# Gates of an expert layer: which one-hot operand is moved, and which stands still

## The chip, the cores and the metric

The program runs on one core of a Trainium2 chip. The metric is the device time in microseconds; lower is better. Each kernel is run several times and the median is taken. One more execution is recorded by the hardware profiler, and all views below are of that one.

The engines are named as in the profile: PE is TensorE (matmuls), PEld its loads of the stationary operand, DVE is VectorE, ACT is ScalarE, POOL is GpSimd, SP is SyncE, which here issues DMA transfers.

## The reference, cut to what matters

Two transformer-like blocks on 256 tokens of width 1024. The last layer is a product-key expert layer: each token chooses 16 of 16,384 experts for each of 8 heads, so 128 experts with a weight each. An expert has a number `first * 128 + second`.

```python
def one(xb):                                   # xb: tokens x 1024
    q = (xb @ wq).reshape(C, PEER_HEADS, 2, PEER_DK_HALF)
    s = jnp.einsum('chpd,hpnd->chpn', q, keys)
    sv, si = lax.top_k(s, K)
    ...
    top_s, sel = lax.top_k(cand.reshape(C, PEER_HEADS, K * K), K)
    eidx = jnp.take_along_axis(cidx.reshape(C, PEER_HEADS, K * K), sel, axis=-1)
    g = jax.nn.softmax(top_s, axis=-1)
    u = u_tab[eidx]
    act = jax.nn.gelu(jnp.einsum('chkd,cd->chk', u, xb), approximate=False)
    w = (g * act).astype(xb.dtype)
    return jnp.einsum('chk,chkd->cd', w, v_tab[eidx])
```

## The kernel before

The kernel does not gather experts. In `peer` it multiplies all 16,384 rows of `u` with all tokens (128 pieces of 128 experts, `u_items`), multiplies each activation by a gate that is zero for experts not chosen, and multiplies the result with all rows of `v` (`v_chunk`). The gates are a tile `G[second number, first number, token]` in float32, and the change is in how it is filled.

**Routing** (`route`) finds for each token its 128 chosen experts and leaves them in `slot[chosen, 5, token]`, in bfloat16: row 0 the first number, row 1 the second, rows 2 to 4 the weight in three parts that add up to it exactly.

**Filling the gates** goes in groups of NB = 4 tokens, 64 groups. `build(t0)` makes one tile `oo[chosen, 5, 128, 4]` on DVE with two instructions. Line 1203 compares the numbers 0 to 127 with the first and the second number of each chosen expert: two sets of one-hot rows, 1024 elements a partition. Line 1204 multiplies the first number's one-hots by the three parts of the weight: 1536 elements. `place(t0)` then does for each of the four tokens three matmuls on PE (line 1212), one for each part of the weight, which add up in PSUM: out[second, first] = sum over the chosen experts of onehot(second) x onehot(first) x weight. The stationary operand is `oo[:, 1, :, j]`, the moving one `oo[:, x, :, j]`, 128 x 128 each. The tokens are the last dimension of `oo`, so that neighbouring columns of an operand are 4 elements, 8 bytes, apart. ACT copies the result of a group into `G` (line 1214). `oo` has two buffers and the PSUM pool `ps_t` three.

**What runs beside it.** `weave(U[NRT:NU], gates(), True)` spreads the 64 builds and 64 places over 53 pieces of `u` (numbers 72 to 124). One piece is: a transfer of 512 KB into `raw` (four buffers, line 127, issued by SP), ACT's copy to a rounded `hi` (line 128, three buffers), DVE's rest `lo` (line 129, two buffers), and 24 matmuls of 256 columns on PE (`mm_a`, lines 139 to 141: `hi` twice, `lo` once). Every second piece ACT applies Gelu (line 1076). The list of gates begins with `build(0)`, and then goes `build(t0 + 4)`, `place(t0)`, so that a build is one place ahead of its own place. By the counts 53 pieces and 64 places, one or two places stand behind a piece. The last argument of `weave` asks that DVE takes up a build only behind the split (line 129) of the same piece. Ahead of this stretch the routing of the first 72 pieces keeps DVE busy; behind it three more pieces follow and then the 128 pieces of `v` (line 1254).

Of the kernel before, what the change touches and what calls it, by code (L numbers as in the profile page):

```python
# [16 lines left out]
OP = mybir.AluOpType  # L17
# [49 lines left out]
def tile_body(ctx, tc, A, out):  # L67
# [12 lines left out]

    # ---- constants
    scratch = tc.tile_pool(name="scratch", bufs=1)
# [33 lines left out]

    # ---- weights: load a piece, split it exactly in two parts of 12 significant bits
    last, crit = [None, None], [None, None]
# [68 lines left out]
    def sum_sq(t, c, o, src, eps):  # L187
        # mean of squares of a row, in two halves
        s = stat[:, t, o:o + 3]
        crit[1] = nc.scalar.activation(sqs, src, AF.Square, accum_out=s[:, c:c + 1])  # L190
        if c == 0:
            nc.vector.tensor_scalar(s[:, 2:3], s[:, 0:1], 1.0 / D, eps, op0=OP.mult, op1=OP.add)
        else:
            nc.vector.tensor_scalar(s[:, 2:3], s[:, 1:2], 1.0 / D, s[:, 2:3], op0=OP.mult, op1=OP.add)
# [24 lines left out]
    def both_norms(t, c, acc):  # L219
        # the residual times the first block's last gain, the means of squares of both, and from these  # L220
        # 1 / rms of the first norm and the product of that with 1 / rms of the norm that follows it
        if c == 0:
            gains["sum", t] = npool.tile([P, D], F32, name="hn")
        a, b, st = gains["sum", t][:, cut(c)], h[t][:, cut(c)], stat[:, t]
        crit[0] = nc.vector.tensor_tensor(a, acc, b, op=OP.add)
        nc.vector.tensor_tensor(b, a, gains["final_g"][:, cut(c)], op=OP.mult)
        sum_sq(t, c, 0, a, EPS)
        sum_sq(t, c, 3, b, 0.0)
        if c:
            nc.vector.scalar_tensor_tensor(st[:, 6:7], st[:, 2:3], EPS, st[:, 5:6], op0=OP.mult, op1=OP.add)  # L230
            nc.vector.tensor_copy(st[:, 7:8], st[:, 2:3])
            nc.gpsimd.tensor_tensor(st[:, 6:8], st[:, 6:8], nhalf[:, :2], op=OP.pow)

    def keep_tiles(pool, n, *names):
        # made when first written; names: slots of tiles that are not read any more by then
        return [lambda name=name: pool.tile([P, 2, PIECE], F32R, name=name, bufs=1)
                for name in [*names, *(f"keep{j}" for j in range(n - len(names)))]]

    def out_proj(src, nk, yT, keep, fin=residual):
        """The last pieces are kept, so that the first tokens are done before the others."""  # L240
        acc = [ps_mm.tile([P, 512], F32, name="mm") for _ in range(4)]
# [31 lines left out]
    def defer(f, n=1):  # L273
        """Emit a step after the n-th of the items that follow."""
        late.append([n, f])
# [17 lines left out]
    def weave(items, side, behind=False):  # L293
        """Emit a list of steps with a list of smaller ones spread between them, by their costs.

        behind: VectorE takes up the smaller ones only behind the split of the step's weights.
        """
        side = [f if isinstance(f, tuple) else (1.0, f) for f in side]
# [16 lines left out]
    def causal(ps, acc, taps, cw, cb):  # L315
        # causal convolution along the tokens; the last tap has no shift
        nc.scalar.activation(acc, ps, AF.Identity, scale=cw[:, taps - 1:taps], bias=cb)  # L317
# [24 lines left out]
    def b_first(src, xT, pool, evac):  # L342
        """A block that begins on the first tokens while the others are still on their way."""
        W = [weight(src[q], 2, keep=pool.tile([P, 2, PIECE], F32R, name=f"keep{q - 2}", bufs=1) if q > 1 else None)
# [9 lines left out]
        def turn(f):  # L354
            # two of its four blocks of columns, columns on partitions
            pt = ps_t.tile([P, 2, T], F32, name="pst")
# [7 lines left out]
    def row_parts(pool, rows, name):  # L364
        # a table that is there twice, at partitions 0 and 32: its first part at 0, its second at 32
        n = rows.shape[0]
# [5 lines left out]
    def rowbc(ps, rows, r, more=None):  # L372
        # one row of a table in two parts, on all partitions; more: a tile to add
        n = rows.shape[0]
# [17 lines left out]

    # ---- layer 0: state space mixer
    def ssd():
        with ExitStack() as es:
# [46 lines left out]
            nc.vector.tensor_scalar(nacs, tk[:, 1], -1.0, None, op0=OP.mult)  # L442
            # large and negative where the position read comes after the position written
            jm = sb.tile([P, P], F32, name="jm")
# [31 lines left out]
            def xs_items(g):  # L476
                # inputs of the recurrence, tokens on partitions
                hs = slice(8 * g, 8 * g + 8)
# [22 lines left out]
            def chain(g):  # L501
                hs = slice(8 * g, 8 * g + 8)
                # decay between every two positions of a chunk, transposed, times the masked products of B and C
                M = {}
# [20 lines left out]
                def state():  # L525
                    # state after the first chunk, read by the second
                    xds = sb.tile([P, 512], F32, name="xds", bufs=2)
# [96 lines left out]
    def fox():  # L624
        with ExitStack() as es:
# [45 lines left out]
            nc.vector.tensor_tensor_scan(cum, one, lf, 0.0, op0=OP.mult, op1=OP.add)  # L671
            # cum is minus the reference's sum
            cumr = row_parts(sb, cum, "cumr")
# [41 lines left out]
            def attend(hg):  # L715
# [3 lines left out]
                def scores(i, pr):  # L719
# [7 lines left out]
                    mx = sb.tile([P, 2], F32, name="mx", bufs=3)  # L727
                    # minus the scores, and minus their maximum
                    for j, hh in enumerate(pr):
# [52 lines left out]
    def mix2():  # L782
        with ExitStack() as es:
# [13 lines left out]

            # convolution branch: some of the taps on the tensor engine, as diagonal matrices
            cT = sb.tile([P, 4, T], F32, name="cT")
# [36 lines left out]

            # low-rank query and key-value parts, tokens on partitions
            cqT = sb.tile([P, 2, 2, T], F32R, name="cqT")
# [12 lines left out]
            def norm_later(src, dst, g, n, then, half=False):  # L851
                # half: the source is twice the row that is meant
                w = src.shape[-1]
# [107 lines left out]
            def scores(i, hh):  # L961
# [4 lines left out]
                mx = sb.tile([P, 1], F32, name="mx", bufs=3)  # L966
                # minus the scores, and minus their maximum
                nc.vector.tensor_tensor_reduce(z[:, :n], sp[:, :n], amask[:, TM - n:], scale=-scale, scalar=-NEG,
# [45 lines left out]
            def conv_done(t):  # L1014
# [12 lines left out]
                def rest():  # L1027
                    nc.vector.scalar_tensor_tensor(ln, ln, r, lb, op0=OP.mult, op1=OP.add)
                    # x (1 + tanh(x / 2)) is twice silu(x)
                    th = sb.tile([P, 512], F32, name="on", bufs=2)  # L1030
# [23 lines left out]
    def peer():  # L1054
        with ExitStack() as es:
# [26 lines left out]
            with ExitStack() as e1:  # L1082
# [8 lines left out]
                def route(t):  # L1091
# [59 lines left out]
                    def finish():  # L1151
# [8 lines left out]
                        for j in range(3):  # L1160
                            nc.tensor.transpose(pt[:, j, :], sl[:, j, :], ident)
                        # a bfloat16 holds a row's number; a weight takes three, which hold it exactly
                        cur = slot[:, :, t * P:(t + 1) * P]
# [33 lines left out]
            iob = const.tile([P, P, NB], BF16, name="metaT")  # L1197
            nc.vector.tensor_copy(iob, iota[:, :, None].to_broadcast([P, P, NB]))

            def build(t0):  # L1200
                oo = wk.tile([P, 5, P, NB], BF16, name="oo", bufs=2)
                cur = slot[:, :, None, t0:t0 + NB].to_broadcast([P, 5, P, NB])
                nc.vector.tensor_tensor(oo[:, :2], iob[:, None].to_broadcast([P, 2, P, NB]), cur[:, :2], op=OP.is_equal)
                nc.vector.tensor_tensor(oo[:, 2:], oo[:, :1].to_broadcast([P, 3, P, NB]), cur[:, 2:], op=OP.mult)  # L1204
                O[t0] = oo

            def place(t0):
                pg = ps_t.tile([P, NB, P], F32, name="pst")
                oo = O.pop(t0)
                for j in range(NB):  # L1210
                    for x in range(2, 5):
                        nc.tensor.matmul(pg[:, j, :], lhsT=oo[:, 1, :, j], rhs=oo[:, x, :, j], start=(x == 2),  # L1212
                                         stop=(x == 4))
                nc.scalar.activation(G[:, :, t0:t0 + NB].rearrange("p i t -> p t i"), pg, AF.Copy)  # L1214
# [8 lines left out]

            # the last groups of four rows of experts come first: they are still on chip
            rows = [4 * n + j for n in (30, 31, *range(30)) for j in range(4)]

            def prepare(k, hi, lo):
                # four rows of experts: activation times gate, in two parts
                i = rows[k]
# [83 lines left out]
def _twice(w):  # L1313
    # columns 0.. and, once more, 32..
    o = np.zeros((w.shape[0], P), w.dtype)
# [80 lines left out]
```

## Time and profile before

| | |
|---|---|
| runs | 1769.67, 1768.04, 1768.36 us; median 1768.36 |
| profiled execution, span | 1767.2 us |
| PE busy | 1728.7 us (98%) |
| PE loads busy | 1536.4 us (87%) |
| DVE busy | 1244.6 us (70%) |
| ACT busy | 973.6 us (55%) |
| line 1212, PE | 768 matmuls, 1160.2 to 1395.9 us |
| granted clock of TensorE, mean | 0.997 |

The span is the time from the first to the last instruction of the profiled execution. Busy time of PE is the union of the matmuls' spans, which overlap one another: a matmul's reported duration is longer than the distance from its start to the next one's. For what a matmul costs in a row of many, the distance is read (the time of a group divided by its count), not the duration. Lines are those of the kernel before; a row shows the line, the engine, the operation, the tiles written and read, the count and the times.

### The profile page before, as it was taken

To read this page: it belongs to the slowest core of one execution; us is meant where nothing else is said; L and a number is where in the kernel's file an instruction comes from. 1 tells how busy PE (TensorE), PEld (TensorE's weight loads), DVE (VectorE), ACT (ScalarE), POOL (GpSimd) and SP (SyncE) were. 2 spreads that over 40 slices of the span, in tenths; PEclk is the share of its full clock that TensorE was granted. 3 is DMA by queue.
4 is the path that set the end of the run, shared out by engine and by line. 5 is a ranking of instruction groups with operands and counts; after the bars stand their busy time and mean duration, and the time that the engine had idled before them with its cause. 6 is when DMAs were issued, how large, how long until landed. Compare 5 with 4: busy or idle time off the path is not lost.

```text
span 1767.2 us, 28831 instructions
## 1 busy us (share of the span) xinstructions
PE 1728.7 (98%) x11035; PEld 1536.4 (87%) x11035; DVE 1244.6 (70%) x2516; ACT 973.6 (55%) x1425; POOL 35.2 (2%) x45
## 2 busy tenths in 40 slices
PE   7999999999999999999999999999999999999998
PEld 6978779987777899878979999999999988888886
DVE  5777667765755677667877999977667666666665
ACT  5778546544465565457854544555555544444443
POOL 0000000000110000000000000000000000000000
PEclk9999999999999999999999999999999999999999
DMA  5534346665454465654245676754454577777774
GB/s 192 175 104 144 119 144 181 189 200 181 131 167 132 125 186 183 204 185 141 80 166 172 214 225 224 224 179 140 142 156 134 167 252 237 237 237 238 238 237 156
DMA packets 87578, 315.29 MB, mean 178 GB/s; under 512 B 9984, under 2 KB 10368, under 8 KB 87312
## 3 DMA queue, kind: packets, MB, share of 16 engines
q1 hardware_dynamic: 80352, 290.36, 52.8%
q10 hardware_dynamic: 7088, 23.09, 3.5%
q8 instruction: 86, 1.41, 0.3%
q14 instruction: 52, 0.43, 0.1%
HBM read 295.59 MB, written 17.83 MB: 177 GB/s over the span
## 4 chain that ended last, share of the span: by engine, by line
PE 91%; DVE 4%; ACT 1%; issue 1%; DMA 1%; POOL 1%; SPq 0%; DVEq 0%; POOLq 0%; ACTq 0%
PE mm L1254 20%; PE mm L139 13%; PE mm L141 13%; PE mm L140 13%; PE mm L146 7%; PE mm L145 7%; PE mm L147 7%; PE pst L1212 5%; DVE lo L129 1%; PE pst L171 1%; PE pst L546 1%; PE pst L724 1%; PE pst L375 1%; PE pst L377 1%; PE po L749 1%
## 5 line engine op out<-in xcount | busy, mean ns | idle before, releaser
L129 DVE TENSOR_TENSOR lo<-raw,hi 128x1024 fp32r<-128x1024 f32 (+1 forms) x492 | 599.9, 1220 | 341.7 <-PE mm L141 112.9
L128 ACT ACTIVATE hi<-raw 128x1024 fp32r<-128x1024 f32 (+1 forms) x492 | 519.3, 1057 | 526.0 <-PE mm L140 242.1
L139 PE MATMUL mm<-xT,hi 128*128 128x256 f32 (+1 forms) x1968 | 562.6, 286 | 1.2 <-DVE cacc L320 1.2
L141 PE MATMUL mm<-xT,lo 128*128 128x256 f32 (+1 forms) x1968 | 557.1, 283 | 1.5 <-DVE lo L129 1.5
L140 PE MATMUL mm<-xT,hi 128*128 128x256 f32 (+1 forms) x1968 | 552.0, 281 | 0.0
L139 PEld LDWEIGHTS mm<-xT,hi 128*128 128x128 f32 x1968 | 373.0, 190 | 5.0 <-issue 2.3
L141 PEld LDWEIGHTS mm<-xT,lo 128*128 128x128 f32 x1968 | 370.7, 188 | 2.6 <-DVE lo L129 2.2
L140 PEld LDWEIGHTS mm<-xT,hi 128*128 128x128 f32 x1968 | 371.8, 189 | 0.5
L1254 PE MATMUL mm<-hi,xT 128*128 128x512 f32 x992 | 270.0, 393 | 0.0
L1254 PEld LDWEIGHTS mm<-hi,xT 128*128 128x128 f32 x992 | 186.3, 188 | 42.6
L1254 PE MATMUL mm<-lo,xT 128*128 128x512 f32 x496 | 154.8, 393 | 0.0
L1254 PEld LDWEIGHTS mm<-lo,xT 128*128 128x128 f32 x496 | 93.1, 188 | 21.7 <-DVE lo L129 0.3
L145 PE MATMUL mm<-hi,xT 128*128 128x512 f32 (+1 forms) x240 | 96.3, 408 | 3.9 <-ACT xT L133 3.8
L1212 PE MATMUL pst<-oo 128*128 128x128 bf16 x768 | 99.4, 297 | 0.0
L147 PE MATMUL mm<-hi,xT 128*128 128x512 f32 (+1 forms) x240 | 95.0, 397 | 2.1 <-DVE xT L134 2.1
L146 PE MATMUL mm<-lo,xT 128*128 128x512 f32 (+1 forms) x240 | 96.1, 400 | 0.7 <-DVE lo L129 0.6
L1212 PEld LDWEIGHTS <-oo 128*128 128x128 bf16 x768 | 83.3, 118 | 3.4
L1214 ACT ACTIVATE G<-pst 128x512 f32<-128x512 f32 x64 | 71.1, 1111 | 16.4 <-PE pst L1212 16.4
L320 DVE SCALAR_TENSOR_TENSOR cacc<-mm,pcol,cacc 128x255 f32<-128x255 f32 (+1 forms) x144 | 68.4, 480 | 13.6 <-ACT cacc L317 11.2
L1204 DVE TENSOR_TENSOR oo<-oo,slot 128x1536 bf16<-128x1536 bf16 x64 | 60.2, 956 | 1.4
L145 PEld LDWEIGHTS mm<-hi,xT 128*128 128x128 f32 x240 | 45.5, 191 | 14.3 <-ACT xT L133 5.4
L147 PEld LDWEIGHTS mm<-hi,xT 128*128 128x128 f32 x240 | 45.5, 190 | 12.3 <-DVE xT L134 4.1
(404 smaller groups left out, 2095.7 us busy)
## 6 DMA issues: line engine op xcount, KB each, us to landing
raw<-in_u SPq DMA_DIRECT2D x128, 512.0 KB, 3.7
raw<-in_v SPq DMA_DIRECT2D x128, 512.0 KB, 4.2
raw<-in_w_up SPq DMA_DIRECT2D x88, 512.0 KB, 3.6
raw<-in_w_dn SPq DMA_DIRECT2D x44, 512.0 KB, 4.2
raw<-in_w_fox SPq DMA_DIRECT2D x32, 512.0 KB, 4.2
spill<-h ACTq DMA_DIRECT2D x30, 512.0 KB, 5.4
h<-spill SPq DMA_DIRECT2D x30, 512.0 KB, 4.7
raw<-in_w_xbc SPq DMA_DIRECT2D x24, 512.0 KB, 3.9
```

Source lines behind the costliest of these rows:

```text
L128: last[1] = nc.scalar.activation(hi[:, :width], raw[:, :width], AF.Copy)
L129: last[0] = nc.vector.tensor_tensor(lo[:, :width], raw[:, :width], hi[:, :width].bitcast(F32), op=OP.subtract)
L139: nc.tensor.matmul(ps, lhsT=hi[:, k, :], rhs=xT[:, k, 0, :], start=(k == 0), stop=False)
L140: nc.tensor.matmul(ps, lhsT=hi[:, k, :], rhs=xT[:, k, 1, :], start=False, stop=False)
L141: nc.tensor.matmul(ps, lhsT=lo[:, k, :], rhs=xT[:, k, 0, :], start=False, stop=(k == nk - 1))
L145: nc.tensor.matmul(ps, lhsT=xT[:, k, 0, c0:c1], rhs=whi, start=first, stop=False)
L146: nc.tensor.matmul(ps, lhsT=xT[:, k, 0, c0:c1], rhs=wlo, start=False, stop=False)
L147: nc.tensor.matmul(ps, lhsT=xT[:, k, 1, c0:c1], rhs=whi, start=False, stop=last)
L320: nc.vector.scalar_tensor_tensor(acc[:, d:], ps[:, :T - d], cw[:, j:j + 1], acc[:, d:], op0=OP.mult, op1=OP.add)
L1212: nc.tensor.matmul(pg[:, j, :], lhsT=oo[:, 1, :, j], rhs=oo[:, x, :, j], start=(x == 2), stop=(x == 4))
L1214: nc.scalar.activation(G[:, :, t0:t0 + NB].rearrange("p i t -> p t i"), pg, AF.Copy)
L1254: nc.tensor.matmul(acc[2 * t + c], lhsT=w[x][:, t * P:(t + 1) * P], rhs=y[:, c, :], start=(i == 0 and x == 0 and y is b[0]), stop=(i == P ...
```

## The change

The roles of the two one-hots are exchanged, and one of them gets another layout. The first number's one-hots are made for the four tokens one after the other, 128 neighbouring elements each, in a view `om` of the first fifth of the tile `oo`; for that the numbers 0 to 127 are also kept once in bfloat16 (`ioc`). The second number's one-hots stay in the old layout, and it is these that are multiplied by the three parts of the weight. In `place` the products are the stationary operand and `om[:, j]` is the moving one. The comparison of 1024 elements becomes two of 512. What is summed for each element of `G` is the same.

```diff
+            ioc = pb.tile([P, P], BF16, name="ioc")
+            nc.vector.tensor_copy(ioc, iota)
...
             def build(t0):
                 oo = wk.tile([P, 5, P, NB], BF16, name="oo", bufs=2)
-                cur = slot[:, :, None, t0:t0 + NB].to_broadcast([P, 5, P, NB])
-                nc.vector.tensor_tensor(oo[:, :2], iob[:, None].to_broadcast([P, 2, P, NB]), cur[:, :2], op=OP.is_equal)
-                nc.vector.tensor_tensor(oo[:, 2:], oo[:, :1].to_broadcast([P, 3, P, NB]), cur[:, 2:], op=OP.mult)
-                O[t0] = oo
+                om = oo[:, 0].rearrange("p a b -> p (a b)").rearrange("p (b a) -> p b a", a=P)
+                cur = slot[:, :, t0:t0 + NB]
+                nc.vector.tensor_tensor(om, ioc[:, None].to_broadcast([P, NB, P]),
+                                        cur[:, 0, :, None].to_broadcast([P, NB, P]), op=OP.is_equal)
+                nc.vector.tensor_tensor(oo[:, 1], iob, cur[:, 1, None].to_broadcast([P, P, NB]), op=OP.is_equal)
+                nc.vector.tensor_tensor(oo[:, 2:], oo[:, 1:2].to_broadcast([P, 3, P, NB]),
+                                        cur[:, 2:, None].to_broadcast([P, 3, P, NB]), op=OP.mult)
+                O[t0] = om, oo

             def place(t0):
                 pg = ps_t.tile([P, NB, P], F32, name="pst")
-                oo = O.pop(t0)
+                om, oo = O.pop(t0)
                 for j in range(NB):
                     for x in range(2, 5):
-                        nc.tensor.matmul(pg[:, j, :], lhsT=oo[:, 1, :, j], rhs=oo[:, x, :, j], start=(x == 2),
-                                         stop=(x == 4))
+                        nc.tensor.matmul(pg[:, j, :], lhsT=oo[:, x, :, j], rhs=om[:, j], start=(x == 2), stop=(x == 4))
```

In the changed kernel the three instructions of a build are lines 1208 (first number), 1210 (second number) and 1211 (products), the matmuls are line 1220, and ACT's copy is line 1221. The rows of PE, ACT, SP and POOL stand in the same order as before. On DVE, a piece with one build and one with two, in the middle of the stretch, stood in this order before (`lo<-raw,hi` is the split of a piece of `u`, `metaT` the slot in which the numbers 0 to 127 lie, each four times):

```order
L129 TENSOR_TENSOR lo<-raw,hi 128x1024
L1203 TENSOR_TENSOR oo<-metaT,slot 128x1024
L1204 TENSOR_TENSOR oo<-oo,slot 128x1536
L129 TENSOR_TENSOR lo<-raw,hi 128x1024
L1203 TENSOR_TENSOR oo<-metaT,slot 128x1024 x2
L1204 TENSOR_TENSOR oo<-oo,slot 128x1536 x2
```

A build is two instructions there, and where two builds stand together both comparisons come ahead of both products. The same two pieces in the changed kernel:

```order
L129 TENSOR_TENSOR lo<-raw,hi 128x1024
L1208 TENSOR_TENSOR oo<-ioc,slot 128x512
L1210 TENSOR_TENSOR oo<-metaT,slot 128x512
L1211 TENSOR_TENSOR oo<-oo,slot 128x1536
L129 TENSOR_TENSOR lo<-raw,hi 128x1024
L1208 TENSOR_TENSOR oo<-ioc,slot 128x512
L1210 TENSOR_TENSOR oo<-metaT,slot 128x512
L1208 TENSOR_TENSOR oo<-ioc,slot 128x512
L1211 TENSOR_TENSOR oo<-oo,slot 128x1536
L1210 TENSOR_TENSOR oo<-metaT,slot 128x512
L1211 TENSOR_TENSOR oo<-oo,slot 128x1536
```

A build is three instructions now; the split stands where it stood, and of two builds the second one's line 1208 comes ahead of the first one's products.

## Rows read from the trace of the kernel before

**Rows 1.** The page: busy time and share; the chain that ended last
```profile
PE 1728.7 (98%) x11035; PEld 1536.4 (87%) x11035; DVE 1244.6 (70%) x2516; ACT 973.6 (55%) x1425; POOL 35.2 (2%) x45
...
PE 91%; DVE 4%; ACT 1%; issue 1%; DMA 1%; POOL 1%; SPq 0%; DVEq 0%; POOLq 0%; ACTq 0%
PE mm L1254 20%; PE mm L139 13%; PE mm L141 13%; PE mm L140 13%; PE mm L146 7%; PE mm L145 7%; PE mm L147 7%; PE pst L1212 5%; DVE lo L129 1%; PE pst L171 1%; PE pst L546 1%; PE pst L724 1%; PE pst L375 1%; PE pst L377 1%; PE po L749 1%
```

**Rows 2.** Tile oo: count, ns min/median/max, first and last start in us, form
```profile
L1212 PEld LDWEIGHTS <-oo x768: 112/117/144, 1160.2 to 1395.9; 128*128 128x128 bf16 x192
L1212 PE MATMUL pst<-oo x768: 284/297/302, 1160.2 to 1396.0; 128*128 128x128 bf16 x192
L1203 DVE TENSOR_TENSOR oo<-metaT,slot x64: 689/693/695, 1153.0 to 1390.6; 128x1024 bf16<-128x1024 bf16 x64
L1204 DVE TENSOR_TENSOR oo<-oo,slot x64: 950/957/959, 1154.2 to 1391.4; 128x1536 bf16<-128x1536 bf16 x64
```

**Rows 3.** Windows: busy us (count) of each engine, PEclk, DMA share, GB/s
```profile
1080.00:1153.00 73.00, 73.00 (x619) 73.00 (x619) 69.83 (x396) 36.70 (x42) 0.00 (x0) 1.00 0.73 228
...
1157.00:1398.00 241.00, 241.00 (x2037) 237.57 (x2037) 166.38 (x181) 140.25 (x144) 0.00 (x0) 1.00 0.48 147
```

**Rows 4.** Waits: who for whom, us in total, times, longest; ACT from 1160, DVE from 1080
```profile
ACT hi L128 <- PE mm L140: 83.4, 52, 1.7
...
DVE lo L129 <- PE mm L141: 48.6, 41, 1.2
...
DVE lo L129 <- issue: 8.2, 15, 1.5
```

**Rows 5.** Chain of waits in order of time, line 1212: start, us, what
```profile
1160.40 1.43 PE pst L1212 x12
1164.66 2.84 PE pst L1212 x24
...
1383.50 2.84 PE pst L1212 x24
...
1393.45 2.86 PE pst L1212 x24
```

**Rows 6.** Line 1254: its part of the chain behind the stretch; one matmul's ns
```profile
1405.11 20.02 PE mm L1254 x86
...
L1254 PE MATMUL mm<-hi,xT x992: 388/392/404, 1416.1 to 1759.5; 128*128 128x512 f32 x199
```

**Rows 7.** Timeline around one group: start us, us, engine, line (loads, matmuls, DVE)
```profile
1201.20 0.19 PEld L141 LDWEIGHTS mm<-xT,lo 128*128 128x128 f32 x1
...
1201.44 1.58 PE L1212 MATMUL pst<-oo 128*128 128x128 bf16 x12
...
1202.73 0.21 PEld L139 LDWEIGHTS mm<-xT,hi 128*128 128x128 f32 x1
1202.98 0.28 PE L140 MATMUL mm<-xT,hi 128*128 128x256 f32 x1
1203.06 0.69 DVE L1203 TENSOR_TENSOR oo<-metaT,slot 128x1024 bf16<-128x1024 bf16 x1
1203.79 0.96 DVE L1204 TENSOR_TENSOR oo<-oo,slot 128x1536 bf16<-128x1536 bf16 x1
```

**Rows 8.** Line 950: four pairs in the timeline; one matmul's ns (smallest: 16 columns)
```profile
836.24 0.36 PE L950 MATMUL pst<-ident,q 16*96 16x16 f32 x4
836.24 0.26 PEld L950 LDWEIGHTS pst<-ident,q 16*96 16x96 f32 x4 [0.36 <-ACT q L943]
...
L950 PE MATMUL pst<-ident,q x24: 192/272/313, 831.7 to 837.3; 128*96 128x128 f32 x16, 16*96 16x16 f32 x8
```

**Rows 9.** DVE: line 528 (ns min/median/max); two of line 1204; line 129 (mean ns)
```profile
L528 DVE TENSOR_TENSOR xds<-xdt,dst x4: 685/692/693, 95.8 to 210.0; 128x512 f32<-128x512 f32 x4
...
1168.14 1.82 DVE L1204 TENSOR_TENSOR oo<-oo,slot 128x1536 bf16<-128x1536 bf16 x2
...
L129 DVE TENSOR_TENSOR lo<-raw,hi 128x1024 fp32r<-128x1024 f32 x52 | 63.7, 1226 | 54.9 <-PE mm L141 48.3 <-issue 6.6
```

## The prediction

> **What bounds the kernel now.** I read the page first, the views of the stretch second. On the page TensorE (PE) is busy for 98% of the span and the chain that ended last is 91% PE, 5% of it in line 1212, the matmuls of `place` [rows 1]. A busy PE is not a PE at its peak, so the question is whether PE waits in the stretch that the change touches, and what one matmul costs there. The 768 matmuls of line 1212 run from 1160.2 to 1395.9 us [rows 2]. In the windows from 1157 to 1398 us PE is busy for all 241.00 us at a granted clock of 1.00, its level of 2.4 GHz, with VectorE (DVE) busy for 166.38, ScalarE (ACT) for 140.25 and the DMA at 147 GB/s [rows 3]. The list of waits has no PE among the waiters there: ACT waits for line 140 for 83.4 us, DVE for line 141 for 48.6 [rows 4]. So whatever PE saves here comes off the span, until another engine is late.
>
> The chain of waits then gives the price. A group of one `place` (12 matmuls) takes 1.43 us, one of two (24) takes 2.84 to 2.86 [rows 5]. There are 52 groups, 40 of one and 12 of two; the first of each and the last two of the pairs stand there. The second `place` of a pair adds 1.41 us, 0.1175 us for one matmul of 128 columns. That number is odd beside its neighbours. In the stretch ahead, from 1080 to 1153 us, PE does 619 matmuls of lines 139 to 141 in 73.00 us without a break [rows 3]: 0.118 us for a matmul of **256** columns. Behind it 86 matmuls of 512 columns take 20.02 us, 0.233 each [rows 6]. A bfloat16 matmul of 128 columns costs as much as one of 256.
>
> **What makes it so.** Two suspects: its load of the stationary operand, or the streaming of its moving one. Both are read with four columns' distance between neighbours (`[..., j]` of a tile whose last dimension is 4), 8 bytes. Loads of line 1212 take 117 ns, the shortest full loads around: those of lines 139 to 141 take 0.19 us and their pairs still go at 0.118 [rows 2, 7]. The matmul itself is reported with 297 ns, against 0.28 us for 256 columns and 0.39 for 512 [rows 2, 6, 7]. With 0.11 us of added length per 256 columns, 297 ns is what 256 to 300 columns would take, not 128. So streaming is slow, about two ticks per column, and I put it down to the distance in the moving operand.
>
> The Trainium skill speaks against that. Its page "SBUF — State Buffer" (section on the DMA port swizzle) says that reads stay at full rate while at least two fall into one 16-byte line, and lets a bfloat16 operand stride up to 8 elements for free; a stride of 4 would then cost nothing. By that rule the 0.1175 us would have another cause and the change would give 0; by the rows it gives the sum below. The rows decide for me, the rule is the second rival.
>
> **The change part by part.**
> 1. *Moving operand contiguous* (`om[:, j]`), 128 columns. From 512 to 256 columns the pitch falls by 0.233 - 0.118 = 0.115 us; half of that again for 256 to 128 gives 0.118 - 0.057 = **0.061 us**. Upper end: 0.1175, no gain. Lower end: four load-and-matmul pairs with loads of 96 columns and only 16 moving columns take 0.36 us, of which the last matmul has 0.19: (0.36 - 0.19) / 3 = 0.056 us a pair [rows 8]; a pair with a full load and 128 columns will hardly beat that. I take 0.061, the value that the two plain rows give.
>  The Trainium skill, "TensorE: Matmul & The Clock Gate", Back-to-back issue gap, gives about 81 ns per matmul for sustained load-and-matmul pairs of 128 columns. By that figure the sum below would be 716 x (0.1175 - 0.081) = 26 us, and the time 1742; no run here shows it.
> 2. *The edges of a group stay.* The load behind a group is one of 0.21 us that begins as the last matmul begins, and the second matmul behind it comes at 1202.98, 0.25 us after that load [rows 7]; this is the load's own length, which no faster streaming shortens. So of 12 matmuls 11 gain, of 24, 23: 40 x 11 + 12 x 23 = 716. Saved: 716 x (0.1175 - 0.061) = **40.5 us**.
> 3. *Stationary operand*: now the three weight parts of the second number, still at a distance of 4, three different ones where there was one loaded three times. Before, it was loaded for every matmul too (768 loads for 768 matmuls [rows 2]), so 0. If loads of three different tiles' columns cost more, they have 0.061 us to hide in.
> 4. *DVE, one more instruction in a build.* Before: 693 ns (1024 elements) + 956 (1536). After: the 1536 stays at 956; the second number's comparison has 512 elements of the old form, and 693 - (956 - 693) = 430 ns; the first number's, 512 elements too, repeats one element of `slot` 128 times as the innermost dimension, which no bfloat16 row here does. Its lower end is the same 430; the nearest row with such an innermost repeat is line 528, 512 elements in float32, 692 ns [rows 9]. I take **690**, since that row has the pattern. A build then costs 0.690 + 0.430 + 0.956 = 2.08 us, 0.43 more, 27 us in 64 builds. All of it lies beside PE, if it fits: 53 splits of 1.226 [rows 9] and 64 builds of 2.08 are 65 + 133 = **198 us**, and PE needs 241 - 40.5 = 200. That is tight as a plain sum. What loosens it: independent DVE instructions overlap (two of line 1204 in 1.82 us, not 1.91 [rows 9]), and so do now line 1208 with the one ahead of it and the next split with line 1211, some 0.09 each, 10 to 15 us in all. What tightens it: a build must wait for the `place` two ahead (two buffers of `oo`), and a step with two builds asks DVE for 1.2 + 4.1 us while PE has 2.84 + 1.5; the next three or four single steps give that back (1.2 + 2.1 against 2.84 + 0.8). The buffers (two of `lo`, four of `raw`) let DVE lag by most of a step. I take 0 for it, and up to 7 us for the range.
> 5. *`ioc`*, one copy of 128 elements, and the first builds, which are longer, ahead of the first `place`: DVE has waits there that end in "issue", up to 1.5 us long [rows 4], so 0, at most 1 us.
> 6. *ACT and DMA*: ACT has 140 us of work in the stretch and 200 to do it. The DMA moves the same bytes in 200 us, 147 x 241 / 200 = 177 GB/s, which it exceeds from 1080 to 1153 us (228 [rows 3]). Both 0. The order of PE's rows does not change. Behind the stretch line 1254 starts after the last splits in both; 0.
>
> Sum: -40.5 us. The profiled execution has a span of 1767.2 us and the median of the runs is 1768.36, 1.2 us more for what lies around it; I keep the 1.2. 1767.2 - 40.5 + 1.2 = **1728 us**.
>
> **The rivals.**
> - *DVE becomes the bound.* PE then waits for builds or splits. For it: 198 against 200 in the plain sum; if every DVE instruction also has the 34 to 40 ns that lie between lines 1203 and 1204 (1203.06 + 0.69 to 1203.79 [rows 7]), 245 x 0.034 = 8 us come on top, 206, and the gain is 35: 1733. If line 1208 costs 1.0 us, 20 us more: 1753. Against it: the overlaps above. Its trace would show PE waiting for line 1210, 1211 or 129.
> - *Nothing changes*: the distance in the moving operand was not the price, but the load (still at a distance of 4) or a fixed price of such pairs. For it: a load's 117 ns are nearly the pitch of 117.5. Against it: loads of 188 ns go at a pitch of 118 next to it, and the matmul's own 297 ns. DVE then has 241 us for 198 and hides. 1768.
> - *In between*: the pair has a floor between 0.061 and 0.1175 that these rows don't show, 0.07 to 0.095 us. 716 x 0.0475 to 716 x 0.0225 is a gain of 34 to 16: 1734 to 1752.
> - *Slower*: line 1208 is far dearer than any row of 512 elements. DVE passes the old 241 us when it takes (241 - 65) / 64 - 1.386 = 1.36 us; at 2.0 it adds 64 x 0.64 = 41 us: 1809. Against it: the rows of 512 elements here stay near 0.69 [rows 9].
>
> **How the numbers follow.** Forecast 0.60: 1728, from 1722 (pitch 0.056 in all) to 1733. Between or DVE-bound 0.22: 1733 to 1753. Nothing 0.12: 1768. Slower 0.04: 1809. A larger gain than 46 us 0.02. Below, I reach to 768 x (0.119 - 0.056) = 48 us, if the edges gain too: 1720. Above, to 1745, which takes in the DVE price of 7 us and the nearer half of the between case. That leaves out nothing (0.12), slower (0.04) and the rest of the between case. A difference of 0.2% (3.5 us) is about what a measurement can tell here: faster 0.83, same 0.13, slower 0.04.
>
> **What would show it.** Right: line 1220 (the old 1212) with 12 matmuls in about 0.81 us and 24 in 1.54 in the chain; matmul durations near 0.23 us; about 200 us from the first to the last `place`; DVE over 90% busy there; line 1208 near 690 ns, 1210 near 430. Streaming wrong: line 1220 still at 0.117 us a matmul. DVE wrong: line 1208 above 0.9 us or PE idle in front of line 1220 or 141. The forecast falls most easily by the pitch of the pair, which is an extrapolation from longer matmuls of another type.

## The result and the profile after

The changed kernel takes 1725.53 us (1722.42 to 1726.47, four runs) against 1769.01 us for the kernel before on the same chip: a ratio of 0.9757, 95% interval 0.9743 to 0.9771. That is 43.5 us less; the profiled executions differ by 44.2 us (spans 1767.2 and 1723.0). The forecast was 1728, from 1720 to 1745.

On the page of the changed kernel PE is as busy as before, 98% of a shorter span, and the gates' matmuls (now line 1220) are 3% of the chain that ended last, where they were 5% [rows 1]. DVE works 15 us more.

```profile
span 1723.0 us, 28885 instructions
...
PE 1684.2 (98%) x11035; PEld 1493.3 (87%) x11035; DVE 1259.5 (73%) x2581; ACT 966.2 (56%) x1425; POOL 35.2 (2%) x45
...
PE 91%; DVE 4%; ACT 1%; issue 1%; DMA 1%; POOL 1%; SPq 0%; DVEq 0%; POOLq 0%; ACTq 0%
```

The view of the tile `oo` has the answer to [rows 2]: count, then shortest, median and longest in ns, then first and last start in us.

```profile
L1220 PEld LDWEIGHTS <-oo x768: 110/113/136, 1159.3 to 1351.5; 128*128 128x128 bf16 x192
L1220 PE MATMUL pst<-oo x768: 219/219/249, 1159.3 to 1351.6; 128*128 128x128 bf16 x192
L1210 DVE TENSOR_TENSOR oo<-metaT,slot x64: 413/418/422, 1152.0 to 1349.3; 128x512 bf16<-128x512 bf16 x64
L1211 DVE TENSOR_TENSOR oo<-oo,slot x64: 948/958/962, 1152.4 to 1349.7; 128x1536 bf16<-128x1536 bf16 x64
L1208 DVE TENSOR_TENSOR oo<-ioc,slot x64: 682/684/693, 1158.3 to 1348.7; 128x512 bf16<-128x512 bf16 x64
```

A matmul is reported with 219 ns instead of 297, its load with 113 instead of 117. What a matmul costs is read from the chain of waits in order of time (start, us, what), as in [rows 5]. A group of one `place` takes 0.70 us, of two 1.37 to 1.38. The second `place` adds 0.675 us for 12 matmuls: 0.056 us each, where it was 0.1175.

```profile
1197.13 0.70 PE pst L1220 x12
1200.73 1.37 PE pst L1220 x24
...
1342.56 1.38 PE pst L1220 x24
1346.83 0.70 PE pst L1220 x12
1350.42 1.37 PE pst L1220 x24
```

The timeline around one group (start us, us, engine, line) answers [rows 7]. There, 1.67 us lay between line 141 ahead of the group, at 1201.31 (the first row below, of the kernel before), and line 140 behind it, at 1202.98; here it is 1197.85 - 1196.85 = 1.00 us.

```profile
1201.31 0.28 PE L141 MATMUL mm<-xT,lo 128*128 128x256 f32 x1
...
1196.85 0.28 PE L141 MATMUL mm<-xT,lo 128*128 128x256 f32 x1
1196.98 0.86 PE L1220 MATMUL pst<-oo 128*128 128x128 bf16 x12
1197.65 0.36 PE L139 MATMUL mm<-xT,hi 128*128 128x256 f32 x1
1197.85 0.28 PE L140 MATMUL mm<-xT,hi 128*128 128x256 f32 x1
```

So a group of one saves 0.67 us, a group of two 0.67 + (1.41 - 0.675) = 1.405, and 40 x 0.67 + 12 x 1.405 = 43.7 us. Within the scatter of the runs this is the whole result: the gain came off the matmuls of line 1220 and nothing gave any of it back. The windows (busy us and count of each engine, PEclk, DMA share, GB/s) show why. In the stretch, now 199 us long, PE is still busy all the time, at a granted clock of 1.00, and DVE for 183.43 us of it, 92%, where it was 166 of 241 [rows 3]. The list of waits has PE waiting for DVE twice, 0.7 us in all.

```profile
1157.00:1356.00 199.00, 198.75 (x2050) 196.31 (x2049) 183.43 (x247) 133.00 (x145) 0.00 (x0) 1.00 0.54 177
...
PE mm L141 <- DVE lo L129: 0.4, 1, 0.4
PE pst L1220 <- DVE oo L1211: 0.3, 1, 0.3
```

### The profile page after: what moved, and what is told of

It is laid out like the page before. It is cut to its first block, busy times and chain, and to the rows that moved or that the text cites. A ratio compares the mean times of both kernels' runs of the same rounds, so it can differ in the third digit from the quotient of the medians.

```text
span 1723.0 us, 28885 instructions
## 1 busy us (share of the span) xinstructions
PE 1684.2 (98%) x11035; PEld 1493.3 (87%) x11035; DVE 1259.5 (73%) x2581; ACT 966.2 (56%) x1425; POOL 35.2 (2%) x45
## 3 DMA queue, kind: packets, MB, share of 16 engines
q8 instruction: 86, 1.41, 0.3%
## 4 chain that ended last, share of the span: by engine, by line
PE 91%; DVE 4%; ACT 1%; issue 1%; DMA 1%; POOL 1%; SPq 0%; DVEq 0%; POOLq 0%; ACTq 0%
PE mm L1261 21%; PE mm L139 13%; PE mm L141 13%; PE mm L140 13%; PE mm L146 7%; PE mm L145 7%; PE mm L147 7%; PE pst L1220 3%; PE pst L171 1%; DVE lo L129 1%; PE pst L546 1%; PE pst L724 1%; PE pst L375 1%; PE pst L377 1%; PE po L749 1%
## 5 line engine op out<-in xcount | busy, mean ns | idle before, releaser
L129 DVE TENSOR_TENSOR lo<-raw,hi 128x1024 fp32r<-128x1024 f32 (+1 forms) x492 | 599.5, 1220 | 299.2 <-PE mm L1261 83.2
L1261 PEld LDWEIGHTS mm<-lo,xT 128*128 128x128 f32 x496 | 93.1, 188 | 21.5
L146 PEld LDWEIGHTS mm<-lo,xT 128*128 128x128 f32 x240 | 45.9, 191 | 9.7 <-DVE lo L129 2.3
L145 PE MATMUL mm<-hi,aT 128*128 128x512 f32 x136 | 53.9, 396 | 0.0
```

Source lines behind the costliest of these rows:

```text
L129: last[0] = nc.vector.tensor_tensor(lo[:, :width], raw[:, :width], hi[:, :width].bitcast(F32), op=OP.subtract)
L145: nc.tensor.matmul(ps, lhsT=xT[:, k, 0, c0:c1], rhs=whi, start=first, stop=False)
L146: nc.tensor.matmul(ps, lhsT=xT[:, k, 0, c0:c1], rhs=wlo, start=False, stop=False)
L1261: nc.tensor.matmul(acc[2 * t + c], lhsT=w[x][:, t * P:(t + 1) * P], rhs=y[:, c, :], start=(i == 0 and x == 0 and y is b[0]), stop=(i == P ...
```

## Experiments on the distance and the roles

The theory was that the price lay in the distance between neighbouring columns of the moving operand. The change does two things at once, it exchanges the roles and it lays one operand out anew; and a load could still be the price. Four kernels separate these. All are edits of the changed kernel, and each ratio is against the kernel before, run on the same chip (1766.97 us).

**The roles exchanged back, the layout kept.**

```diff
-   nc.tensor.matmul(pg[:, j, :], lhsT=oo[:, x, :, j], rhs=om[:, j], ...)
+   nc.tensor.matmul(pg[:, j, :], lhsT=om[:, j], rhs=oo[:, x, :, j], ...)
```

> The changed kernel with the two operands of the gates' matmuls exchanged again: the contiguous one-hots of the first number stand still, the products, 8 bytes apart, are moved. The gates come out with first and second number exchanged. All DVE work is as in the changed kernel. Theory (the distance between moving columns is the price): 0.1175 us a matmul again, group of 12 at 1.43 us, time back at 1768 +- 3. Rival (the load of the strided stationary operand was the price): the load is contiguous now, so about 0.056 us a matmul and 1726. The longer DVE work should cost nothing here, since PE needs 241 us for the stretch and DVE under 200.

Measured: 1764.74 us, ratio 0.9991 (0.9981 to 1.0). The load reads neighbours now and the moving operand does not, and the old time is back, so the load's distance was not the price. The loads are reported with 96 to 118 ns, 115 in the median; why most of them stay that long with neighbours to read is not shown. The chain has 1.39 us for a group of one and 2.79 for two, 1.40 / 12 = 0.117 us for a matmul. A group of one is 0.04 us shorter than in [rows 5] and a group of two 0.05, 40 x 0.04 + 12 x 0.05 = 2.2 us in all, which is the difference between this kernel and the one before; the interval reaches up to no difference.

```profile
1158.10 1.39 PE pst L1220 x12
1162.33 2.79 PE pst L1220 x24
```

**The roles kept, the layout of before.**

```diff
-   om = oo[:, 0].rearrange("p a b -> p (a b)").rearrange("p (b a) -> p b a", a=P)
+   om = oo[:, 0]
...
-   nc.vector.tensor_tensor(om, ioc[:, None].to_broadcast([P, NB, P]), cur[:, 0, :, None].to_broadcast([P, NB, P]), op=OP.is_equal)
+   nc.vector.tensor_tensor(om, iob, cur[:, 0, None].to_broadcast([P, P, NB]), op=OP.is_equal)
...
-   rhs=om[:, j]
+   rhs=om[:, :, j]
```

> The changed kernel's roles (first number moved, products standing still) with the old layout for both, moving columns 4 elements (8 bytes) apart; the copy of the numbers and the slow comparison go, the first number's comparison is a second one of the old form. Theory (distance): 0.1175 us a matmul, 1768 +- 3. Rival (it was the exchange of roles, three different loads instead of one address three times, that brought the gain): 0.056 us a matmul, 1726.

Measured: 1767.56 us, ratio 1.0003 (0.9994 to 1.0013). The exchange of roles by itself is worth nothing. The groups in the chain are those of the kernel before:

```profile
1201.04 1.43 PE pst L1217 x12
1205.30 1.43 PE pst L1217 x12
1209.57 2.84 PE pst L1217 x24
```

**A distance of 2 elements, 4 bytes.** The first number's one-hots lie in two halves of two tokens each.

```diff
+   om = oo[:, 0].rearrange("p a b -> p (a b)").rearrange("p (h a b) -> p h a b", h=2, a=P)
+   first = slot[:, 0, t0:t0 + NB].rearrange("p (h b) -> p h b", h=2)
+   nc.vector.tensor_tensor(om, iob[:, None, :, :2].to_broadcast([P, 2, P, 2]), first[:, :, None].to_broadcast([P, 2, P, 2]), op=OP.is_equal)
...
+   rhs=om[:, j // 2, :, j % 2]
```

> The changed kernel with the first number's one-hots in two halves of two tokens, so that moving columns are 2 elements (4 bytes) apart. float32 columns, 4 bytes apart too, are streamed at 0.118 us for 256, so the theory that a column is free up to 4 bytes and doubled at 8 says 0.056 us a matmul and 1725 +- 3. If any distance doubles a bfloat16 column: 0.1175 and 1768. The comparison of the first number should fall from 684 to about 418 ns, which moves nothing, since PE sets the stretch.

Measured: 1725.48 us, ratio 0.9769 (0.9753 to 0.9786). The chain has 0.74 and 1.46 us, so 0.72 / 12 = 0.060 us a matmul, a few ns more than with neighbours. The comparison of the first number falls from 684 to 418 ns, and the time does not show it.

```profile
1199.98 1.46 PE pst L1219 x24
1204.32 0.74 PE pst L1219 x12
...
L1207 DVE TENSOR_TENSOR oo<-metaT,slot x64: 411/418/422, 1151.2 to 1349.3; 128x512 bf16<-128x512 bf16 x64
```

**A distance of 8 elements, 16 bytes.** The one-hots of both numbers are interleaved in the first two fifths of the tile.

```diff
+   both = oo[:, :2].rearrange("p n a b -> p (n a b)").rearrange("p (a n b) -> p n a b", n=2, b=NB)
+   om = both[:, 0]
+   nc.vector.tensor_tensor(om, iob, cur[:, 0, None].to_broadcast([P, P, NB]), op=OP.is_equal)
+   nc.vector.tensor_tensor(both[:, 1], iob, cur[:, 1, None].to_broadcast([P, P, NB]), op=OP.is_equal)
...
+   rhs=om[:, :, j]
```

> The changed kernel with moving columns 8 elements (16 bytes) apart: the one-hots of both numbers lie interleaved. If the price is two ticks for whatever does not lie close enough: 0.1175 us a matmul, 1768 +- 3. If it grows with the distance (four ticks): 0.22 to 0.23 us a matmul, group of 12 at 2.7, 716 x 0.11 = 79 us more, 1847. By a rule of 16-byte lines with two reads in each, 8 bytes would be free and 16 not; the changed kernel's gain already speaks against it.

Measured: 1904.76 us, ratio 1.0781 (1.0756 to 1.0806). The chain has 2.77 us for a group of one and 5.55 for two, so 2.78 / 12 = 0.232 us a matmul. The price grows with the distance. Neighbours, 4, 8 and 16 bytes cost 0.056, 0.060, 0.1175 and 0.232 us for 128 columns.

That accounts for 40 x (2.77 - 1.43) + 12 x (5.55 - 2.84) = 86 us, the size that was expected (79). But the time rose by 138, to 1905 and not to the 1847 expected. The other 52 us are in none of the theories; the windows show where they are.

```profile
1159.40 2.77 PE pst L1218 x12
1166.52 5.55 PE pst L1218 x24
...
1157.00:1540.00 383.00, 383.00 (x2081) 301.01 (x2080) 176.02 (x245) 142.88 (x147) 0.00 (x0) 0.84 0.28 94
...
1404.82 0.41 PE L140 MATMUL mm<-xT,hi 128*128 128x256 f32 x1
1405.03 0.41 PE L141 MATMUL mm<-xT,lo 128*128 128x256 f32 x1
...
1408.14 0.28 PE L141 MATMUL mm<-xT,lo 128*128 128x256 f32 x1
1408.26 0.28 PE L139 MATMUL mm<-xT,hi 128*128 128x256 f32 x1
```

The granted clock is 0.84 on the mean of the stretch, though PE was busy in all of its 383.00 us. The two levels are 1.0 and 0.5, so 0.32 of the stretch, 122 us, ran at 1.2 GHz. The ordinary matmuls of 256 columns behind a group (from 1404.82 on, with a group of 12 at 0.23 us ahead of them) come every 0.21 us with a duration of 0.41, and later in the same piece every 0.12 with 0.28. 122 / 0.213 = 573 such matmuls lose 0.095 us each, 54 us: the missing part. This takes all the time at the lower clock to lie in ordinary matmuls, and by the trace nearly all does: the granted clock is 0.98 in the group from 1402.10 to 1404.70 us, 0.50 behind it from 1404.80 to 1407.90, and 1.00 again from 1408.10 and in the next group. The groups themselves take 2.77 us throughout. That the slow streaming ahead is what lowered the clock is suggested by the order of events and by the clock of 0.99 to 1.00 in the same stretch of every kernel here with 8 bytes or less; no run here tested it apart.

## Experiments on the load and on DVE's room

These four ran beside the kernel before at 1767.16 us.

**The load reads neighbours too.** The stationary operand is read as 128 neighbouring elements of the products, which belong to several tokens and not to one.

```diff
-   lhsT=oo[:, x, :, j]
+   lhsT=oo[:, x].rearrange("p a b -> p (a b)")[:, j * P:(j + 1) * P]
```

> The changed kernel, but the stationary operand is read as 128 neighbouring elements of the same products, so that no operand has a distance. It holds the wrong elements: the gates are not the reference's. Theory (a load's distance costs nothing as long as the load is hidden behind the matmul ahead): loads at 113 ns and 0.056 us a matmul as in the changed kernel, 1725 +- 3. Rival (the distance in the load costs something that still shows): a shorter load, a shorter first step of a group (83 ns now), at most 52 x 0.03 = 1.5 us, which would hardly be seen in the time, only in the rows.

Measured: 1723.97 us, ratio 0.9756 (0.974 to 0.9772). The view of the line: loads fall from 113 to 98 ns, the matmuls keep their 219.

```profile
L1220 PEld LDWEIGHTS <-oo x768: 96/98/99, 1157.2 to 1348.5; 128*128 128x128 bf16 x192
L1220 PE MATMUL pst<-oo x768: 219/219/230, 1157.2 to 1348.5; 128*128 128x128 bf16 x192
...
1194.88 0.69 PE pst L1220 x12
1198.46 1.36 PE pst L1220 x24
```

A group gains 0.01 to 0.02 us (0.69 and 1.36). A load's distance costs 15 ns, and the matmul ahead hides it, except at a group's first step. The two kernels cannot be told apart by their times.

**DVE does the slow comparison twice.** Line 1208 stands twice in each build.

> The changed kernel with the first number's comparison (line 1208, 684 ns) done twice in every build. It asks how much room DVE has left. DVE waited for 12 of 199 us in the changed kernel's stretch. 64 x (0.684 - 0.085) = 38 us more work, less the 12: about 26 us longer, 1751, with PE waiting for DVE. If DVE still hides: 1725.

Measured: 1741.96 us, ratio 0.9854 (0.9837 to 0.987). DVE is the bound for the most part: it is busy for 216.16 of 217 us, its lines make up 52% of the chain from 1160 to 1340 us, with line 1213 (line 1211 in the changed kernel) at 16%, and PE waits for it. But the time rose by 16.4 us over the changed kernel's 1725.53 (17.0 between the profiled spans) and not by 26, so DVE had more room than the 12 us of waits that were counted.

```profile
1157.00:1374.00 217.00, 207.81 (x2050) 199.25 (x2049) 216.16 (x312) 134.38 (x146) 0.00 (x0) 1.00 0.50 162
...
PEld L1222 <- DVE oo L1213: 8.3, 12, 1.6
```

**A third of the gates' matmuls.**

```diff
-   for x in range(2, 5):
+   for x in (2,):
```

> The changed kernel with one of the three matmuls for each token, the first part of the weight alone; the gates lack the two smaller parts. It asks what the next gain on PE would be worth. 512 matmuls of 0.056 us are 28.7 us. If PE stays the bound: 1697. Theory (DVE is next, 12 us behind): the stretch cannot get shorter than DVE's work, 199 - 12 = 187 us, so about 1713, with PE waiting for builds or splits.

Measured: 1703.59 us, ratio 0.9637 (0.9621 to 0.9653): 21.9 us less than the changed kernel (21.4 between the profiled spans), where PE alone would give 28.7 and the expectation was 12. DVE is at its end, 177.46 of 179 us. That it alone set this stretch is not shown: the few waits of PE itself are put down to ACT's copies to `hi`, 3.4 us, and hardly to DVE, 0.2, and why those copies came late was not followed further.

```profile
1157.00:1336.00 179.00, 175.10 (x1543) 169.75 (x1542) 177.46 (x247) 132.39 (x145) 0.00 (x0) 1.00 0.57 195
...
PE mm L139 <- ACT hi L128: 3.4, 7, 0.5
```

The same 64 builds keep DVE busy for 177 us here and for 183 in the changed kernel. The timeline of DVE says how. The edit touches none of DVE's instructions, but they stand in another order. Line 1211 needs line 1210's result. In the changed kernel it comes right behind it in 51 of the 64 builds, 0.46 us after its start. Here it does so once; in the others a split (51 times) or another comparison (12) stands between them and starts 0.34 us after line 1210.

```profile
1241.09 0.42 DVE L1210 TENSOR_TENSOR oo<-metaT,slot 128x512 bf16<-128x512 bf16 x1
1241.55 0.96 DVE L1211 TENSOR_TENSOR oo<-oo,slot 128x1536 bf16<-128x1536 bf16 x1
1242.42 1.22 DVE L129 TENSOR_TENSOR lo<-raw,hi 128x1024 fp32r<-128x1024 f32 x1
...
1240.28 0.42 DVE L1210 TENSOR_TENSOR oo<-metaT,slot 128x512 bf16<-128x512 bf16 x1
1240.62 1.22 DVE L129 TENSOR_TENSOR lo<-raw,hi 128x1024 fp32r<-128x1024 f32 x1
1241.75 0.95 DVE L1211 TENSOR_TENSOR oo<-oo,slot 128x1536 bf16<-128x1536 bf16 x1
```

The first three rows are of the changed kernel, the last three of this one. The order does not follow from how busy DVE is: the changed kernel keeps its own also where DVE goes on without a pause, as here, where the split starts at 1242.42 before line 1211 is through. So 0.12 us in each of 51 builds, the 6 us between 183 and 177, hang on the order of the instructions. The doubled comparison stands between the dependent pair in the same way, and there DVE's busy time rose by 216.16 - 183.43 = 33 us and not by 38. In its own order, DVE has 199 - 183 = 16 us of room in the changed kernel; with another order, as in these two kernels, about 20.

**Neighbours without the exchange of roles.** The products themselves are laid out token by token and moved, the second number's one-hots stand still as in the kernel before.

```diff
+   pr = oo[:, 2:].rearrange("p x a b -> p x (a b)").rearrange("p x (b a) -> p x b a", a=P)
+   nc.vector.tensor_tensor(pr, om[:, None].to_broadcast([P, 3, NB, P]), cur[:, 2:, :, None].to_broadcast([P, 3, NB, P]), op=OP.mult)
...
+   nc.tensor.matmul(pg[:, j, :], lhsT=oo[:, 1, :, j], rhs=pr[:, x - 2, j], ...)
```

> The roles of before (second number stands still, the first number's products are moved), but the products are laid out one token after the other, so that the moving columns are neighbours. No exchange of roles at all. PE should go at 0.056 us a matmul, as in the changed kernel. DVE pays: the products repeat an element of the weight 128 times as the innermost dimension, 1536 elements at one a tick, 0.15 + 1.60 = 1.75 us in place of 0.957, a build 0.684 + 0.418 + 1.75 = 2.85 us. 53 splits and 64 builds with overlaps are 60 + 172 = 232 us and more with waits, against 199 of PE: DVE sets the stretch, 1758 to 1770. If PE set it: 1725.

Measured: 1753.88 us, ratio 0.9929 (0.9913 to 0.9946), 4 us under the range expected. The products take 1.75 us as expected, DVE is busy for 227.37 of 228 us, and the products are 46% of the chain in the stretch. This is the rival "DVE becomes the bound", brought about by the edit: the matmuls, line 1221 here, are reported with the 219 ns of the changed kernel, and two thirds of the gain are lost.

```profile
L1221 PE MATMUL pst<-oo x768: 217/219/311, 1160.1 to 1381.3; 128*128 128x128 bf16 x192
L1212 DVE TENSOR_TENSOR oo<-oo,slot x64: 1739/1749/1755, 1158.3 to 1378.7; 128x1536 bf16<-128x1536 bf16 x64
...
1157.00:1385.00 228.00, 208.68 (x2034) 198.81 (x2033) 227.37 (x246) 135.48 (x143) 0.00 (x0) 0.99 0.47 152
```

## Why the prediction was right

**What bounds the kernel**: right. PE was busy in the whole stretch and stayed so, and its groups account for 43.7 us, where the runs differ by 43.5 and the profiled executions by 44.2.

**The cause**: right, and now shown. The layout without the exchange of roles (in the last experiment) speeds the matmuls up, the exchange without the layout does not, and a load that reads neighbours gives nothing. The reading that decided it ahead was the right one: 297 ns for 128 columns beside 0.28 us for 256, with the shorter load.

**The rule that spoke against it** fails for this operand. The Trainium skill, "SBUF — State Buffer" (section on the DMA port swizzle), lets a bfloat16 operand stride up to 8 elements for free as long as two reads fall into a 16-byte line. At 8 bytes two columns do, and a matmul took 0.1175 us in place of 0.056; at 16 bytes 0.232. The measurement decides: for the moving operand of TensorE only up to 4 bytes were nearly free here.

**The pitch**: 0.061 us forecast, 0.056 measured. The extrapolation from 512 and 256 columns of float32 was 5 ns too dear, 716 x 0.005 = 3.6 us, about the difference between 40.5 us forecast and 43.7 found. The lower bound, 0.056 from the pairs of line 950 [rows 8], is the number that was met; those pairs move only 16 columns, so the agreement may be chance, and no run here shows that one thing sets both. The Trainium skill's figure of about 81 ns for such pairs ("TensorE: Matmul & The Clock Gate", Back-to-back issue gap), which would have given 1742, was too high here: 0.056 us with a load in every pair.

**The edges of a group**: 0.67 us were saved in a group of 12, against 11 x 0.0565 = 0.62 forecast. The sum is nearly right because two small misses cancel. The last step was said to be the load's own length, which nothing shortens; but the load has 0.21 us in [rows 7], the step 0.25, and it fell to 0.23. The first step of a group, on the other hand, gained only 0.025 us (the starts of its first two matmuls lie 0.108 us apart before and 0.083 after, in the median), and the ten steps between 0.062 each.

**The stationary operand**: right. Three different loads in place of one repeated cost nothing, and their distance 15 ns that are hidden.

**DVE**: the durations were right (684, 418 and 958 ns for 690, 430 and 956 forecast), the sum too (198 less 10 to 15; busy 183.43), and so was the value of 0 for it. What I had as tight, 198 against 200, had in fact 16 us of room, and about 20 with the other order of DVE's instructions that the doubled comparison and the third of the matmuls have. The rival stood where it was put, though: 38 us more DVE work and it decides.

**ACT and DMA**: 133.00 us of 199 and 177 GB/s, the number forecast; neither holds PE up.

## What to carry to other kernels

When a matmul of few columns costs as much as one of twice as many next to it, look at how far apart its moving columns lie; the layout of the moving operand was worth 43 us here, that of the stationary one too little to be seen in the time. Whoever then moves the layout work to another engine should sum up that engine's work against the shortened stretch, not against the old one: laid out on the wrong side of the product, the same contiguity cost two thirds of the gain, through DVE's longer products. Where one operand must be repeated or multiplied, let the one whose distance is hidden, the stationary one, carry the products.

## What the runs showed of the hardware that I had not expected

- The price of a moving column about doubled from 4 to 8 bytes and again from 8 to 16: 0.060, 0.1175 and 0.232 us for 128 bfloat16 columns at 4, 8 and 16 bytes, 0.056 for neighbours.
- With 16 bytes the granted clock of TensorE fell to 0.84 over the stretch though PE was busy throughout, and the unchanged matmuls of 256 columns behind the slow groups took 0.21 us in place of 0.12. About 52 of the 138 us lost came from there and not from the slow matmuls themselves.
- A load of a stationary operand whose columns lie 8 bytes apart took 113 ns, of neighbours 98, and of 128 float32 columns 188. Of the 15 ns between the first two only the first step of a group shows anything.
- On DVE, line 1211 started 0.46 us after line 1210, whose result it needs, and an instruction that does not need it 0.34 us after. The same builds and splits took 177 us of DVE's time where something stood between the two, and 183 where mostly nothing did.
